# Where a transposed projection tile puts its 512-column and its 256-column products, and how the mixer's column tiles are summed

## The chip, the core and the metric

The kernel runs on one core of one Trainium2 chip. The metric is device time in microseconds (us) of one execution. The median of three runs of the kernel before is 892.92 us (892.76 to 893.49).

## What is computed

Two layers of a decoder trunk over 256 tokens (S) of 1024 channels (D). Each layer is a SwiGLU feed-forward block (FFN), a token mixer, and a second FFN, each followed by a layer norm:

```python
for l in range(DEPTH):                                   # DEPTH = 2, D_FF = 2816
    f = swiglu(x, ffn_w_gate[l, 0], ffn_w_up[l, 0], ffn_w_down[l, 0])
    x = layer_norm(ALPHA * x + 0.5 * f, ln_g[l, 0], ln_b[l, 0])
    z = x @ w_in[l]
    y_a = mixer_spatial_gating(z[..., :512], ...)        # heads A
    y_b = mixer_short_conv(z[..., 512:1280], ...)        # B: gate, gate, input
    y_c = mixer_rglru(z[..., 1280:], ...)                # C: gate, recurrent input
    y = jnp.concatenate([y_a, y_b, y_c], axis=-1) @ w_out[l]
    x = layer_norm(ALPHA * x + y, ln_g[l, 1], ln_b[l, 1])
    f = swiglu(x, ffn_w_gate[l, 1], ffn_w_up[l, 1], ffn_w_down[l, 1])
    x = layer_norm(ALPHA * x + 0.5 * f, ln_g[l, 2], ln_b[l, 2])
```

## The kernel before

**Arithmetic.** Every float32 operand is kept as two parts, a rounded high part and the rest as a low part, and a product is the sum of three: high by high, high by low and low by high. For weights the parts are the buffers `wh` and `wl`; for the activations, transposed so that channels lie on partitions, they are `xT[k, 0]` and `xT[k, 1]`, 256 columns each, side by side, for each of the KD = 8 blocks of 128 channels. `xTb` is the same tensor with both parts taken as one row of 512 columns.

**Weights.** They come from memory as blocks of 128 x 1024. For each block `stream` (L408) issues a DMA into one of 6 `raw` buffers, ScalarE rounds it into one of 12 `wh` buffers, and VectorE subtracts to fill the `wl` of the same number. So the two engines can be up to 12 blocks ahead of TensorE.

**Products with columns of weights (T tiles).** A block of 128 output channels is one tile: `sub_T` (L466) walks over the 8 values of k and calls a step that takes the weights as the stationary operand and `xT` as the moving one. There are two steps:

- `mm_TT` (L440), in the FFNs. A *joined* product of 512 columns (`wh` by both parts of `xT[k]`) fills a whole PSUM bank of 512 columns, and a *single* product of 256 columns (`wl` by the high part) adds to its first half. For k = 0 to 6 the joined one comes first; for k = 7 the two are swapped, so that the joined one closes the bank. Here J is a joined product and s a single one: a tile runs J s J s ... J s, then s J.
- `mm_T` (L434), in the mixers' column tiles: three products of 256 columns for each k, all into the first half of a bank.

In an FFN `total` (L452) then copies the second half of the bank out with ScalarE and adds the first half with VectorE. The 154 T tiles of the four FFNs are 40 in the first FFN and 38 in each of the others; the first FFN begins with `first_unit` (L625), which runs four tiles at once, one pair for each of four banks in turn, and the others begin with *nat* tiles (moving weights, activations stationary) and have two groups of three transposes among their first T tiles. After the T tiles comes `down` (L518): products of 512 columns into four banks, three for each block and half.

**Mixers.** Each of the two has 12 column tiles, made by `col` (L723) and used by `xr_sub`, `g_sub`, `c_sub`, `x_sub` and `b_sub`, which read the finished first half of the bank straight from PSUM. Among the column tiles stand `ri_sub` (L740), products of the convolved `xr`, `sgu` (L783), and transposes. The results go to `yTh` and `yTl`, the operands of the mixer's own `down`; its last input, channel block 7, is the result of `b_sub(1)`.

**Order.** The kernel records its operations with estimated costs, dependences and due times, and `issue` (L212) writes out one fixed order for each engine from them: TensorE by program order where operands are ready, VectorE and ScalarE by the earliest due time. Each engine then runs its list strictly in order. A product counts as columns plus 16, at 2.4 columns a nanosecond, whatever stands beside it.

Of the kernel before, what the change touches and what calls it, by code (L numbers as in the profile page):

```python
# [13 lines left out]
ALU = mybir.AluOpType  # L14
# [4 lines left out]
S = 256  # L19
L = 2  # L20
DFF = 2816
KD = D // P
# [256 lines left out]
def build(tc, a):  # L279
# [7 lines left out]
    def ap(v, dtype=None):  # L287
        return v.ap(dtype) if isinstance(v, View) else v
# [4 lines left out]
    def act(out, in_, func, scale=1.0, bias=0.0):  # L293
        ptrs = len(views(scale, bias))
        cost = in_.n / 1.2 + (50 if in_.psum else 92) + 93 * ptrs
        pr.add("A", cost, views(in_, scale, bias), [out], lambda: A.activation(  # L296
            out=ap(out), in_=ap(in_), func=func, scale=ap(scale), bias=ap(bias)))

    def tt(out, in0, in1, op, eng="V", as32=False, cost=None):
        cost = cost or out.n / 0.96 + 69  # L300
        e = V if eng == "V" else G
        pr.add(eng, cost, [in0, in1], [out], lambda: e.tensor_tensor(  # L302
            out=ap(out), in0=ap(in0), in1=ap(in1, F32 if as32 else None), op=op))
# [13 lines left out]
    def copy(out, in_):  # L317
        act(out, in_, AF.Copy)
# [5 lines left out]
    def walk(x):  # L324
        return x.rearrange("p (a b c) -> p b a c", b=RUNS, c=RUN)

    def mm(out, lhsT, rhs, start, stop, cost=None, runs=None, both=False):

        cost = cost or (out.n + 16) / 2.4

        def go():
            o, x = ap(out), ap(rhs)
            if runs is not None:
                x = walk(x)[:, runs]
                o = walk(o) if both else o
            T.matmul(out=o, lhsT=ap(lhsT), rhs=x, start=start, stop=stop)  # L336
        pr.add("T", cost, [lhsT, rhs], [out], go)
# [13 lines left out]
    def buf(name, shape, dtype=F32, pool=None, **kw):  # L351
        b = Buf(name, shape, dtype, phase=opened.get(pool), **kw)
        (cbufs if pool is None else phases[pool]).append(b)
        return b
# [21 lines left out]
    xT = buf("xT", (KD, 2, S), F32R, off=OFF_X)  # L376
    xTb = xT.alias((KD, 2 * S))
# [19 lines left out]
    def bank(*shape):  # L397
        b = bank_fifo.pop(0)
        return b.alias(shape) if shape else b
# [8 lines left out]
    def stream(upto, part=None):  # L408
        assert upto <= pos["blk"] + RING
        while loaded["n"] < min(upto, nblk):  # L410
            i = loaded["n"]
            r, h, l = raw[i % RAW], wh[i % RING], wl[i % RING]
            sl = slice(0, D) if part is None else slice(part * 512, part * 512 + 512)
            dma(r[sl], a["w"][i][:, sl])
            split(h[sl], l[sl], r[sl])
            if part == 0:
                return
            loaded["n"] += 1

    def take(n):  # L420
        b = pos["blk"]
        pos["blk"] += n
        stream(pos["blk"])
        return list(range(b, b + n))


    ALL = slice(0, RUNS)
# [12 lines left out]
    def mm_TT(b, h, l, k):  # L440


        def joined(stop):
            mm(b.all, h, xTb[k, :], k == 0, stop, runs=ALL, both=True)

        if k < KD - 1:
            joined(False)
        mm(b[:S], l, xT[k, 0, :], False, False, runs=ALL, both=True)
        if k == KD - 1:
            joined(True)  # L450

    def total(out, b):  # L452

# [12 lines left out]
    def sub_T(out, blk, step=mm_T):  # L466
        i = blk % RING
        for k in range(KD):
            ks = slice(k * P, (k + 1) * P)
            step(out, wh[i][ks], wl[i][ks], k)  # L470
# [91 lines left out]
    def ffn(layer, i, ln_prev, nxt, mid=None):  # L562
# [35 lines left out]
        for j, (kind, c0, n) in enumerate(units):  # L598
            if kind == "nat":
                continue  # L600
            f, m = c0 // P, n // P
            if kind == "first":
                first_unit(take(4), th, hh, hTh, hTl)
                continue
            b = take(2 * m)
            for q in range(m):
                pg = bank()
                sub_T(pg, b[q], mm_TT)
                total(hh[q, :], pg)
            act(th[:m, :], hh[:m, :], AF.Tanh, scale=0.5)  # L610
            stt(th[:m, :], th[:m, :], 1.0, hh[:m, :], ALU.add, ALU.mult)
            for _ in range(2):
                if todo:
                    hT(*todo.pop(0))
            for q in range(m):
                pu = bank()
                sub_T(pu, b[m + q], mm_TT)
                total(hh[q, :], pu)
            tt(hh[:m, :], th[:m, :], hh[:m, :], ALU.mult)
            split(hTh[f:f + m, :], hTl[f:f + m, :], hh[:m, :])  # L620
            if mid and j == 3:
                mid()
        return down(hTh, hTl, NF, TAIL, 4.0 * ALPHA, 16.0 * EPS, last, nxt)

    def first_unit(b, th, hh, hTh, hTl):  # L625

        accs = [bank() for _ in range(4)]
        for k in range(KD):
            i = b[k // 2] % RING
            for j in range(4):  # L630
                cs = slice((k % 2) * 512 + j * P, (k % 2) * 512 + (j + 1) * P)
                mm_TT(accs[j], wh[i][cs], wl[i][cs], k)
        for j in range(2):
            total(hh[j, :], accs[j])
            act(th[j, :], hh[j, :], AF.Tanh, scale=0.5)
            stt(th[j, :], th[j, :], 1.0, hh[j, :], ALU.add, ALU.mult)
            total(hh[j, :], accs[2 + j])
            tt(hh[j, :], th[j, :], hh[j, :], ALU.mult)
            split(hTh[j, :], hTl[j, :], hh[j, :])


    def mixer(layer, ln_prev, nxt):
# [3 lines left out]
        def mbuf(n, *shape, dtype=F32, **kw):  # L646
            return buf(n, shape, dtype, name, **kw)
# [15 lines left out]
        e2 = mbuf("e2", 4, S)  # L663
        cc = mbuf("cc", 2, S)
        cy = mbuf("cy", 2, S)
        gn = e2.alias((4, 256))
        vst = [mbuf(f"vst{h}", 6) for h in range(2)]
        vmv = [mbuf(f"vmv{h}", 2) for h in range(2)]
# [53 lines left out]

        def col():  # L723
            b = bank()
            sub_T(b[:S], take(1)[0])
            return b

        def g_sub(k):
            b = col()
            act(gT[k, :], b[:S], AF.Gelu_apprx_tanh)  # L730
            unbank(b)

        def xr_sub(k):
            b = col()
            act(xr[k, :], b[:S], AF.Identity, scale=pc(PW + k * 4 + 3), bias=pc(PB + k))
            for j in range(1, 4):
                stt(xr[k, j:], b[:S - j], pc(PW + k * 4 + 3 - j), xr[k, j:], ALU.mult, ALU.add)
            unbank(b)
# [25 lines left out]
        def c_sub(k):  # L764
            b = col()
            copy(cc[k, :], b[:S])
            unbank(b)
# [96 lines left out]
    b = bank()  # L864
# [15 lines left out]
    for layer in range(L):  # L880
        ln = ffn(layer, 0, ln, (layer, 1), derive if layer == 0 else None)
        ln = mixer(layer, ln, (layer, 2))
        ln = ffn(layer, 1, ln, (layer + 1, 0) if layer + 1 < L else None)
# [108 lines left out]
```

## Time and profile before

| | us |
|---|---|
| median of three runs | 892.92 |
| the profiled execution | 893.46 |
| its span, first to last instruction | 891.4 |
| TensorE (PE) busy | 882.3 |
| its weight loads (PEld) busy | 781.0 |
| VectorE (DVE) busy | 654.7 |
| ScalarE (ACT) busy | 483.9 |

The profiled execution lies 0.54 us above the median, and 2.06 us of it are outside the span. A product's "us" in the profile is from its start to its modelled end, which overlaps the next one's start; what a product costs the engine is the distance from its start to the start of the next. The timeline merges neighbours of one kind into one row (x2), so that the swap at the end of a tile shows as a row of two singles and a row of two joined ones.

### The profile page before, as it was taken

To read this page: it belongs to the slowest core of one execution; us is meant where nothing else is said; L and a number is where in the kernel's file an instruction comes from. 1 tells how busy PE (TensorE), PEld (TensorE's weight loads), DVE (VectorE), ACT (ScalarE), POOL (GpSimd) and SP (SyncE) were. 2 spreads that over 40 slices of the span, in tenths; PEclk is the share of its full clock that TensorE was granted. 3 is DMA by queue.
4 is the path that set the end of the run, shared out by engine and by line. 5 is a ranking of instruction groups with operands and counts; after the bars stand their busy time and mean duration, and the time that the engine had idled before them with its cause. 6 is when DMAs were issued, how large, how long until landed. Compare 5 with 4: busy or idle time off the path is not lost.

```text
span 891.4 us, 13272 instructions
## 1 busy us (share of the span) xinstructions
PE 882.3 (99%) x5068; PEld 781.0 (88%) x5068; DVE 654.7 (73%) x971; ACT 483.9 (54%) x707; POOL 22.3 (3%) x33
## 2 busy tenths in 40 slices
PE   9999999999999999999999999999999999999996
PEld 7888888889988888888888888888999888888885
DVE  6999775497898777764697777646979887777515
ACT  6785564267745656644455665543676466555410
POOL 0000000011000000000000000000200000000000
PEclk9999999999999999999999999999999999999999
DMA  8996555467358555555385555553853575555401
GB/s 311 375 314 228 190 192 205 171 221 252 118 187 277 198 189 189 191 206 194 131 281 202 190 195 193 201 190 125 320 208 112 195 271 190 194 201 195 142 1 47
DMA packets 51903, 178.11 MB, mean 200 GB/s; under 512 B 6144, under 2 KB 7936, under 8 KB 51840
## 3 DMA queue, kind: packets, MB, share of 16 engines
q1 hardware_dynamic: 51840, 177.28, 57.3%
q8 instruction: 39, 0.64, 0.3%
q14 instruction: 24, 0.20, 0.1%
HBM read 176.20 MB, written 1.05 MB: 199 GB/s over the span
## 4 chain that ended last, share of the span: by engine, by line
PE 97%; DMA 1%; DVE 1%; SPq 0%; ACT 0%; issue 0%; DVEq 0%
PE bank L336 96%; PE bank L340 1%; DMA raw<-w 1%; DMA x0t<-xT 1%; SPq L346 0%; DVE xn L314 0%; DVE wl L302 0%; ACT wh L296 0%; DVE st L488 0%; DVEq L988 0%; DVE mv L493 0%; DVE ve L309 0%
## 5 line engine op out<-in xcount | busy, mean ns | idle before, releaser
L302 DVE TENSOR_TENSOR wl<-raw,wh 128x1024 fp32r<-128x1024 f32 (+1 forms) x320 | 385.5, 1209 | 155.2 <-ACT wh L296 154.0
L336 PE MATMUL bank<-xT,wh 128*128 128x512 f32 (+1 forms) x1648 | 492.8, 363 | 0.2 <-DVE xT L302 0.2
L296 ACT ACTIVATE wh<-raw 128x1024 fp32r<-128x1024 f32 (+1 forms) x320 | 333.8, 1048 | 235.2 <-PE bank L336 218.4
L336 PE MATMUL bank<-xT,wl 128*128 128x256 f32 x1456 | 377.8, 277 | 0.4 <-DVE wl L302 0.4
L336 PEld LDWEIGHTS bank<-xT,wh 128*128 128x128 f32 x1648 | 285.4, 188 | 38.8 <-DVE xT L302 0.9
L336 PEld LDWEIGHTS bank<-xT,wl 128*128 128x128 f32 x1456 | 273.7, 188 | 12.5 <-DVE wl L302 1.3
L336 PE MATMUL bank<-wl,hTh 128*128 128x512 f32 (+1 forms) x374 | 138.2, 369 | 0.0
L336 PE MATMUL bank<-wh,hTh 128*128 128x512 f32 (+1 forms) x374 | 137.9, 369 | 0.0
L336 PE MATMUL bank<-wh,hTl 128*128 128x512 f32 (+1 forms) x374 | 137.9, 369 | 0.0
L296 ACT ACTIVATE hh<-bank 128x256 f32<-128x256 f32 x158 | 56.5, 374 | 78.2 <-PE bank L336 73.5
L302 DVE TENSOR_TENSOR hh<-bank,hh 128x256 f32<-128x256 f32 x158 | 64.2, 419 | 26.7 <-ACT hh L296 26.6
L336 PEld LDWEIGHTS bank<-wl,hTh 128*128 128x128 f32 x374 | 70.2, 188 | 10.8
L336 PEld LDWEIGHTS bank<-wh,hTh 128*128 128x128 f32 x374 | 70.3, 188 | 10.7
L336 PEld LDWEIGHTS bank<-wh,hTl 128*128 128x128 f32 x374 | 70.2, 188 | 10.6
L336 PE MATMUL bank<-wh,xT 128*128 128x512 f32 (+1 forms) x320 | 79.3, 334 | 0.0
L336 PEld LDWEIGHTS bank<-wh,xT 128*128 128x128 f32 x320 | 54.9, 188 | 6.5 <-DVE xT L302 0.6
L336 PE MATMUL bank<-wl,xT 128*128 128x512 f32 (+1 forms) x160 | 53.0, 331 | 0.0
L314 DVE SCALAR_TENSOR_TENSOR xn<-xn,bank 128x512 f32<-128x512 f32 (+1 forms) x25 | 16.2, 663 | 38.2 <-PE bank L336 38.2
L302 POOL TENSOR_TENSOR rs<-ve,mhalf 128x1 f32<-128x1 f32 x16 | 13.8, 863 | 863.5 <-DVE ve L309 863.5
L336 PEld LDWEIGHTS bank<-wl,xT 128*128 128x128 f32 x160 | 30.1, 188 | 3.1
L296 ACT ACTIVATE hTh<-hh 128x512 fp32r<-128x512 f32 (+1 forms) x42 | 25.4, 605 | 8.4 <-DVE hh L302 8.2
L302 DVE TENSOR_TENSOR hh<-th,hh 128x512 f32<-128x512 f32 (+1 forms) x42 | 27.7, 660 | 1.2
(93 smaller groups left out, 470.3 us busy)
## 6 DMA issues: line engine op xcount, KB each, us to landing
raw<-w SPq DMA_DIRECT2D x312, 512.0 KB, 4.1
gB<-ln_g SPq DMA_DIRECT2D x6, 512.0 KB, 6.5
bB<-ln_b SPq DMA_DIRECT2D x6, 512.0 KB, 6.4
raw<-w SPq DMA_DIRECT2D x8, 256.0 KB, 5.1
x0t<-xT SPq DMA_DIRECT2D x8, 128.0 KB, 4.6
xn<-x SPq DMA_DIRECT2D x2, 512.0 KB, 6.1
out<-xn SPq DMA_DIRECT2D x3, 256.0 KB, 2.0
wT<-sgu_wT SPq DMA_DIRECT2D x2, 256.0 KB, 6.8
```

What stands on the lines that cost most here:

```text
L296: pr.add("A", cost, views(in_, scale, bias), [out], lambda: A.activation(out=ap(out), in_=ap(in_), func=func, scale=ap(scale), bias=ap(bias)))
L302: pr.add(eng, cost, [in0, in1], [out], lambda: e.tensor_tensor(out=ap(out), in0=ap(in0), in1=ap(in1, F32 if as32 else None), op=op))
L314: pr.add("V", cost, views(in0, s, in1), [out], lambda: V.scalar_tensor_tensor(out=ap(out), in0=ap(in0), scalar=ap(s), in1=ap(in1), op0=op0 ...
L336: T.matmul(out=o, lhsT=ap(lhsT), rhs=x, start=start, stop=stop)
L340: pr.add("T", 109.0, [in_, ident.all], [out], lambda: T.transpose(out=ap(out), in_=ap(in_), identity=ap(ident.all)))
```

## The change

`mm_TT` loses its swap: every k issues the joined product, then the single one, and the closing mark moves to the single one of k = 7. The mixers' `col` uses `mm_TT` instead of `mm_T`. Since its result then lies in both halves of the bank and its users read the first half alone, ScalarE copies the second half into a new buffer `low` of 256 columns (one for all twelve tiles), and VectorE adds it onto the first half, in PSUM.

```diff
     def mm_TT(b, h, l, k):
-        def joined(stop):
-            mm(b.all, h, xTb[k, :], k == 0, stop, runs=ALL, both=True)
-
-        if k < KD - 1:
-            joined(False)
-        mm(b[:S], l, xT[k, 0, :], False, False, runs=ALL, both=True)
-        if k == KD - 1:
-            joined(True)
+        mm(b.all, h, xTb[k, :], k == 0, False, runs=ALL, both=True)
+        mm(b[:S], l, xT[k, 0, :], False, k == KD - 1, runs=ALL, both=True)
...
+        low = mbuf("low", S)
...
         def col():
             b = bank()
-            sub_T(b[:S], take(1)[0])
+            sub_T(b, take(1)[0], mm_TT)
+            copy(low.all, b[S:])
+            tt(b[:S], b[:S], low.all, ALU.add)
             return b
```

In the built program, TensorE around the end of a T tile of the first FFN (the bank's name changes where the next tile begins; 32x4 is the joined product, 16x4 the single one), before:

```order
L336 MATMUL bank_103<-xT,wh_86 128x4x32x4
L336 MATMUL bank_103<-xT,wl_98 128x4x16x4 x2
L336 MATMUL bank_103<-xT,wh_86 128x4x32x4
L336 MATMUL bank_104<-xT,wh_75 128x4x32x4
L336 MATMUL bank_104<-xT,wl_87 128x4x16x4
```

and, as a piece of the difference at the end of the four interleaved tiles of `first_unit`:

```order
+L336 MATMUL bank_100<-xT,wh_78 128x4x32x4
 L336 MATMUL bank_100<-xT,wl_90 128x4x16x4
-L336 MATMUL bank_100<-xT,wh_78 128x4x32x4
+L336 MATMUL bank_101<-xT,wh_78 128x4x32x4
 L336 MATMUL bank_101<-xT,wl_90 128x4x16x4
```

The neighbouring two singles and the two joined products are gone everywhere; TensorE's products alternate without a break.

VectorE in the first mixer, around the convolution of the second `xr` tile (bank_103; bank_105 is the column tile g3, `wl` are weight splits), before:

```order
L302 TENSOR_TENSOR wl_89<-raw_70,wh_77 128x1024
L314 SCALAR_TENSOR_TENSOR xr<-bank_103,prm,xr 128x255
L314 SCALAR_TENSOR_TENSOR xr<-bank_103,prm,xr 128x254
L314 SCALAR_TENSOR_TENSOR xr<-bank_103,prm,xr 128x253
L302 TENSOR_TENSOR wl_90<-raw_71,wh_78 128x1024
```

and after:

```order
L302 TENSOR_TENSOR bank_103<-bank_103,low 128x256
L314 SCALAR_TENSOR_TENSOR xr<-bank_103,prm,xr 128x255
L302 TENSOR_TENSOR bank_105<-bank_105,low 128x256
L314 SCALAR_TENSOR_TENSOR xr<-bank_103,prm,xr 128x254
L302 TENSOR_TENSOR wl_90<-raw_71,wh_78 128x1024
L314 SCALAR_TENSOR_TENSOR xr<-bank_103,prm,xr 128x253
```

The three multiply-adds on `xr` stood together, ahead of the split; now an addition for a later tile and the split stand between them.

VectorE at the end of the first mixer (cc and cy belong to the B heads, bank_104 and bank_101 are the two `b_sub` tiles), before:

```order
L314 SCALAR_TENSOR_TENSOR cy<-cc,prm,cy 128x255
L302 TENSOR_TENSOR yTl<-cc,yTh 128x256
L314 SCALAR_TENSOR_TENSOR cy<-cc,prm,cy 128x254
L302 TENSOR_TENSOR wl_97<-raw_72,wh_85 128x1024
L302 TENSOR_TENSOR cc<-cy,bank_101 128x256
L302 TENSOR_TENSOR wl_98<-raw_73,wh_86 128x1024
L302 TENSOR_TENSOR yTl<-cc,yTh 128x256
```

and after:

```order
L314 SCALAR_TENSOR_TENSOR cy<-cc,prm,cy 128x255
L302 TENSOR_TENSOR cc<-cy,bank_104 128x256
L314 SCALAR_TENSOR_TENSOR cy<-cc,prm,cy 128x254
L302 TENSOR_TENSOR bank_101<-bank_101,low 128x256
L302 TENSOR_TENSOR yTl<-cc,yTh 128x256
L302 TENSOR_TENSOR cc<-cy,bank_101 128x256
L302 TENSOR_TENSOR wl_97<-raw_72,wh_85 128x1024
L302 TENSOR_TENSOR yTl<-cc,yTh 128x256
```

The added addition stands ahead of the last `yTl`, and one weight split has moved behind it.

## Rows read from the trace of the kernel before

**Rows 1.** The page: span, and busy time of each engine.

```profile
span 891.4 us, 13272 instructions
PE 882.3 (99%) x5068; PEld 781.0 (88%) x5068; DVE 654.7 (73%) x971; ACT 483.9 (54%) x707; POOL 22.3 (3%) x33
...
PE 97%; DMA 1%; DVE 1%; SPq 0%; ACT 0%; issue 0%; DVEq 0%
```

**Rows 2.** Waits of PE: for whom, total us, times, longest.

```profile
PE bank L336 <- DVE zero L863: 1.3, 1, 1.3
PE bank L336 <- DVE wl L302: 0.4, 2, 0.2
```

**Rows 3.** Groups by line and shape: xcount | busy us, mean ns | idle.

```profile
L336 PE MATMUL bank<-xT,wh 128*128 128x512 f32 x1264 | 424.3, 388 | 0.2 <-DVE xT L302 0.2
L336 PE MATMUL bank<-xT,wh 128*128 128x256 f32 x384 | 68.6, 280 | 0.0
```

**Rows 4.** Timeline of PE, first FFN (start, us, engine, line, operation).

```profile
100.27 0.28 PE L336 MATMUL bank<-xT,wl 128*128 128x256 f32 x1
100.38 0.38 PE L336 MATMUL bank<-xT,wh 128*128 128x512 f32 x1
100.60 0.28 PE L336 MATMUL bank<-xT,wl 128*128 128x256 f32 x1
...
102.27 0.39 PE L336 MATMUL bank<-xT,wl 128*128 128x256 f32 x2
102.50 0.64 PE L336 MATMUL bank<-xT,wh 128*128 128x512 f32 x2
102.97 0.28 PE L336 MATMUL bank<-xT,wl 128*128 128x256 f32 x1
...
103.44 0.40 PE L336 MATMUL bank<-xT,wh 128*128 128x512 f32 x1
103.67 0.28 PE L336 MATMUL bank<-xT,wl 128*128 128x256 f32 x1
...
105.29 0.60 PE L336 MATMUL bank<-xT,wh 128*128 128x512 f32 x2
...
107.96 0.64 PE L336 MATMUL bank<-xT,wh 128*128 128x512 f32 x2
```

**Rows 5.** Timeline of PE in first_unit, and the first wait behind it.

```profile
13.05 0.28 PE L336 MATMUL bank<-xT,wl 128*128 128x256 f32 x1
...
15.13 0.28 PE L336 MATMUL bank<-xT,wl 128*128 128x256 f32 x1
...
18.20 0.38 PE L336 MATMUL bank<-xT,wl 128*128 128x256 f32 x1 [0.16 <-DVE wl L302]
```

**Rows 6.** Timeline of PE, second FFN: after three transposes.

```profile
284.62 0.28 PE L336 MATMUL bank<-xT,wl 128*128 128x256 f32 x1
...
285.98 0.28 PE L336 MATMUL bank<-xT,wl 128*128 128x256 f32 x1
...
286.65 0.39 PE L336 MATMUL bank<-xT,wl 128*128 128x256 f32 x2
...
287.35 0.28 PE L336 MATMUL bank<-xT,wl 128*128 128x256 f32 x1
...
289.10 0.28 PE L336 MATMUL bank<-xT,wl 128*128 128x256 f32 x1
```

**Rows 7.** Timeline of PE: the first mixer's last two column tiles, and down.

```profile
236.39 0.39 PE L336 MATMUL bank<-xT,wh 128*128 128x256 f32 x2
...
239.14 0.39 PE L336 MATMUL bank<-xT,wh 128*128 128x256 f32 x2
...
241.89 0.38 PE L336 MATMUL bank<-wh,yTh 128*128 128x512 f32 x1
```

**Rows 8.** Groups by shape: a copy and an addition as the change adds them.

```profile
L296 ACT ACTIVATE hh<-bank 128x256 f32<-128x256 f32 x158 | 56.5, 374 | 78.2 <-PE bank L336 73.5 <-DVE hTl L302 2.1 <-DVE sp L309 1.2
L302 DVE TENSOR_TENSOR hh<-bank,hh 128x256 f32<-128x256 f32 x158 | 64.2, 419 | 26.7 <-ACT hh L296 26.6
```

**Rows 9.** The first mixer's column tiles: us, busy of PE, PEld, DVE, ACT.

```profile
203.51:241.89 38.38, 38.38 (x322) 37.95 (x321) 29.70 (x56) 27.82 (x46) 3.75 (x4) 1.00 0.53 185
```

**Rows 10.** Timeline of DVE, then of PE: two results and their users.

```profile
214.19 1.51 DVE L314 SCALAR_TENSOR_TENSOR xr<-bank,prm,xr 128x255 f32<-128x255 f32 x3
...
249.37 0.42 DVE L302 TENSOR_TENSOR yTl<-cc,yTh 128x256 fp32r<-128x256 f32 x1
...
218.64 0.59 PE L336 MATMUL bank<-xr,wa 128*128 128x256 f32 x2
...
250.91 0.38 PE L336 MATMUL bank<-wh,yTl 128*128 128x512 f32 x1
```

## The prediction, made before the changed kernel ran

> **What bounds the kernel now.** I read the busy shares first, then PE's waits, then the starts of single products. PE is busy for 882.3 of 891.4 us, and the chain that ended last is PE for 97% [rows 1]. It waits for next to nothing: 1.3 us for the first zeros and 0.4 us for weights at the start [rows 2]. So a product's column count, and what two neighbouring products do to each other, set the time; the other engines matter only where they come late. What the reader must see is the distance between starts. In one T tile joined products start 0.22 us and singles 0.11 us before their successors (100.27, 100.38, 100.60), and the six pairs from 100.27 to 102.27 take 2.00 us, 0.3333 us each [rows 4]. In the next tile a joined product takes 0.23 to 0.24 us (103.44 to 103.67) without any wait. The rows of two joined products stand 2.79 us apart across the slow tile (102.50 to 105.29) and 2.67 us across the fast one (105.29 to 107.96), 5.46 us for two tiles, and this alternation runs on to the end of each FFN: of the 154 T tiles 74 are slow, 69 fast and 11 irregular (beside transposes, or the first ones of an FFN).
>
> **When a tile turns slow.** It turns at the swap. Two singles in a row pass at once, and the two joined products behind them (102.50 to 102.97) take 0.47 us where twice 0.22 would be 0.44 [rows 4]; from there the pairs stay slow until the next swap throws them back. In the fast tile all pairs between the swaps keep 0.3333 us exactly. So there are at least two steady ways to run the same pair; a swap kicks PE out of the good one, and the next one happens to kick it back. After any other disturbance the good one is found within a few pairs: behind three transposes the four pairs from 284.62 to 285.98 take 1.36 us, 0.03 over, and from there PE keeps the good pace up to the swap at 286.65 [rows 6]. Ten such entries stand in the trace (one in the first FFN, three in each of the others); all reach the good pace within 8 pairs.
>
> **Term 1, the FFNs.** The change removes the swaps and adds no instruction. If the good pace, once found, lasts across tiles, a tile costs 8 x 0.3333 = 2.667 us. Two tiles then take 5.333 us instead of 5.46: 69 slow-fast couples give 69 x 0.127 = 8.8 us. The five slow tiles beyond these give about 0.11 each, 0.6 us, and the irregular ones lose a swap or one late entry, 0.2 us (an estimate from the 0.03 us of the joined pair at the swap). That is 9.5 us. Nothing behind it becomes late: VectorE and ScalarE wait for PE to free weight buffers, not the other way [rows 2], and 1% more pace is far from their busy shares [rows 1]. What could break the pace at a tile's border is the new bank and the jump back from k = 7 to 0; the swapped border has both as well, and behind a slow tile it begins the good pace (105.29), so I price them at nothing.
>
> A rule speaks against this whole term. The Trainium skill, "TensorE: Matmul & The Clock Gate", in "Part 2: What happens when you issue a matmul", says that the next weights are loaded through a read port of their own and take no bandwidth from the running product. By that rule 512 and 256 columns would cost the same in any order and term 1 would be zero. The trace disagrees as far as two tiles of equal columns and no wait differ by 0.12 us [rows 4], though it does not show why.
>
> **Term 2, PE in the mixers' column tiles.** 384 products of 256 columns, two for each of 24 x 8 pairs [rows 3], become 192 of 512, and singles stay. An undisturbed column tile takes 2.75 us now (236.39 to 239.14 to 241.89) [rows 7] against 2.667: 24 x 0.083 = 2.0 us. Seven of twelve tiles begin behind something else (transposes, `ri_sub`, `sgu`, the nat tiles) and pay the entry of 0.03 to 0.04 us: 14 x 0.035 = 0.5 us. Net gain 1.5 us; bounds 0 (if none finds the pace) and 2.0.
>
> **Term 3, the sum put back.** Each column tile adds a copy on ACT, 374 ns, and an addition on DVE, 419 ns by the same shape from PSUM to SBUF [rows 8]; none here writes PSUM, so I take 0.42 with 0.35 and 0.6 as ends. Over 38.38 us of column tiles ACT goes from 27.8 to 32.3 us and DVE from 29.7 to 34.7 [rows 9], 84% and 90%: it fits in total. It lengthens each chain from a column tile by 0.8 to 0.9 us, and the queues are strict. Two places are tight. The second `xr` was ready at 214.19 + 1.51 = 215.70 and used at 218.64 [rows 10], 2.9 us of slack. Now its last multiply-add stands behind the addition for g3 and a weight split: from g3's end about 0.45 (copy) + 0.42 + 0.48 + 1.22 + 0.48 = 3.1 us, and PE comes to it after one `ri_sub` and one tile, 0.67 + 2.86 = 3.5 us. Just covered. The last `yTl` was ready at 249.79 and used at 250.91, 1.1 us of slack [rows 10]. Its list on DVE has an addition and a multiply-add more ahead of it and one split less, and starts some 0.4 us later behind ScalarE's three added copies, while PE arrives 0.2 us earlier. I work this out to a stall of 0.2 to 0.4 us; with the other tight joints I take 0.4 us in each mixer, 0.8 in all, bounds 0 and 3. The three splits pushed behind are needed tens of us later. A bank is held 0.8 us longer, of eight, with a tile each 2.7 us: nothing.
>
> **The sum.** 9.5 + 1.5 - 0.8 = 10.2 us off the profiled execution's 893.46 gives 883.3; off the median, 0.54 lower, 882.7 us. With the bounds of terms 2 and 3 on the good side, and 0.3 us more for term 1 (its rows are rounded to 0.01 us), 881.1; with terms 2 and 3 on the bad side 886.4.
>
> **Rivals.**
>
> *The slow steady pace everywhere.* The only place of before where J and s alternate for longer than a tile is `first_unit`, and there six pairs from 13.05 to 15.13 take 2.08 us, 0.3467 each, steadily, until the swaps end it [rows 5]. If the changed stream ran so, 154 tiles would take 154 x 2.773 = 427.1 us against 421.6 now (74 x 2.78 + 69 x 2.68 + 11 irregular ones of 2.8 on average), 5.5 us more; mixers gain nothing and stall 0.8: 899.2 us, slower. It decides if an FFN's last entry lands there; then no swap frees it. Against it: ten of the eleven entries reached the good pace. For it: the pattern is the very one.
>
> *The slow pace in one or two of the four FFNs.* Each costs 34 tiles x 8 x 0.0133 = 3.6 us: 886.3 or 889.9 us.
>
> *The pace is lost at every border and found again.* Then each tile pays something between 0.03 us [rows 6] and the slow tile's 0.11, much what the mean tile pays today (5.46 / 2 - 2.667 = 0.063): 892 us, from 887 to 900.
>
> *Order is not the cause.* Slow tiles could follow the odd-numbered weight buffers, which they mostly do. Then terms 2 and 3 alone remain, 892.2 us. This is also where the skill's rule above leads. Against it, in the second FFN the tile that by the built order uses weight buffer 4 is a slow one, five pairs from 287.35 to 289.10 in 1.75 us [rows 6], where in the first FFN even buffers are fast; the step sits at the swap, not with the buffer.
>
> **How the numbers follow.** The forecast 62%, 881.1 to 886.4. The slow pace in one or two FFNs 14%. Lost at the borders 12%, split over faster, same and slower as 5, 3 and 4. The slow pace everywhere 8%, order not the cause 4%. A measurement of this kernel tells about 0.2%, 1.8 us, from no change: faster 62 + 14 + 5 = 81%, same 3 + 4 = 7%, slower 4 + 8 = 12%. The range that holds 8 in 10 runs from 881.1 to 891.0, the forecast, the partly slow case and the better half of the border case.
>
> **What the profile of after would show.** Right: the starts of the first singles of consecutive T tiles 2.67 us apart all along, no row x2 of joined products in a T tile, 107 us for the first FFN's T tiles, column tiles of 2.67 us, PE waiting below 1 us in a mixer. Wrong: pairs of 0.347 us in long runs (the slow pace), or 0.3333 broken at each change of bank. Waits of PE for `xr` or `yTl` over 0.5 us would break term 3. The clock was granted in full in that stretch, 1.00 [rows 9]; a lower one would void all of it.

## The result: 882.28 us, a ratio of 0.9884

| | before | after |
|---|---|---|
| median of three runs, us | 892.92 (892.76 to 893.49) | 882.28 (882.01 to 883.76) |
| the profiled execution, us | 893.46 | 883.76 |
| its span, us | 891.4 | 881.7 |

The ratio is 0.9884, with a 95% interval of 0.9861 to 0.9906. The forecast was 882.7 us. The profiled execution of the changed kernel is the slowest of its three; for it the sum gave 883.3 us.

The page of the changed kernel, span and busy times, beside [rows 1]:

```profile
span 881.7 us, 12928 instructions
PE 872.1 (99%) x4876; PEld 770.9 (87%) x4876; DVE 658.5 (75%) x995; ACT 491.4 (56%) x731; POOL 22.3 (3%) x33
```

TensorE still bounds the kernel. It has 192 instructions fewer (384 products of 256 columns became 192 of 512) and 10.2 us less busy time. Its waits (for whom, total us, times, longest), beside [rows 2]:

```profile
PE bank L336 <- DVE zero L860: 1.2, 1, 1.2
PE bank L336 <- DVE wl L302: 0.7, 2, 0.5
PE bank L336 <- DVE xT L302: 0.4, 1, 0.4
```

Next the timeline of TensorE in the first FFN (start, us, engine, line, operation), beside [rows 4]. Three tiles begin at 99.75, 102.42 and 105.08; the second pair of the first begins at 100.08. No row of that stretch shows x2 any more:

```profile
99.75 0.38 PE L336 MATMUL bank<-xT,wh 128*128 128x512 f32 x1
...
100.08 0.38 PE L336 MATMUL bank<-xT,wh 128*128 128x512 f32 x1
...
102.42 0.38 PE L336 MATMUL bank<-xT,wh 128*128 128x512 f32 x1
...
105.08 0.38 PE L336 MATMUL bank<-xT,wh 128*128 128x512 f32 x1
...
107.75 0.38 PE L336 MATMUL bank<-xT,wh 128*128 128x512 f32 x1
```

A pair takes 0.33 us and eight of them 2.667 (99.75 to 107.75 is 24 pairs in 8.00 us), where the swaps at the ends of a slow and a fast tile stood 2.79 and 2.67 apart [rows 4]. Where the time went is shown by the stretches of T tiles in the four FFNs, from the first tile behind `first_unit` or the first T tile to the first product of `down` (us, then busy us and count of PE, PEld, DVE, ACT and POOL, granted clock, DMA share, GB/s), before:

```profile
17.66:127.36 109.70, 109.54 (x641) 96.73 (x640) 98.43 (x176) 73.91 (x116) 0.00 (x0) 1.00 0.77 270
281.32:385.75 104.43, 104.43 (x616) 92.58 (x615) 78.90 (x110) 61.47 (x98) 0.00 (x0) 1.00 0.59 204
461.89:566.39 104.50, 104.50 (x616) 92.65 (x615) 78.91 (x110) 61.48 (x98) 0.00 (x0) 1.00 0.60 204
720.32:824.75 104.43, 104.43 (x616) 92.61 (x615) 78.90 (x110) 61.47 (x98) 0.00 (x0) 1.00 0.59 205
```

and after, with the column tiles of the first mixer as a last line:

```profile
17.58:125.08 107.50, 107.00 (x642) 96.34 (x641) 98.19 (x176) 74.81 (x116) 0.00 (x0) 1.00 0.79 278
278.64:380.85 102.21, 102.21 (x617) 92.26 (x616) 78.08 (x111) 61.60 (x98) 0.00 (x0) 1.00 0.59 209
457.01:559.17 102.16, 102.16 (x617) 92.24 (x616) 78.08 (x110) 61.53 (x98) 0.00 (x0) 1.00 0.60 209
712.87:815.04 102.17, 102.17 (x617) 92.22 (x615) 78.06 (x111) 61.56 (x98) 0.00 (x0) 1.00 0.59 208
...
201.23:238.91 37.68, 37.68 (x227) 33.88 (x226) 30.97 (x63) 30.70 (x57) 3.80 (x5) 1.00 0.55 188
```

The four FFNs lose 2.20, 2.22, 2.34 and 2.26 us, 9.0 together, with the same products and the same clock. The mixer's tiles lose 38.38 - 37.68 = 0.70 us [rows 9]. The added operations, by shape (count, busy us, mean ns, idle before them), beside [rows 8]:

```profile
L302 DVE TENSOR_TENSOR bank<-bank,low 128x256 f32<-128x256 f32 x24 | 10.2, 424 | 0.8 <-ACT low L296 0.8
...
L296 ACT ACTIVATE low<-bank 128x256 f32<-128x256 f32 x24 | 9.0, 375 | 3.5 <-DVE ra L302 1.9 <-DVE bank L302 1.6
```

### The profile page after: what moved, and what is told of

It reads as the page before. It is cut to its first block, busy times and chain, and to the rows that moved or that the text cites. A ratio compares the mean times of both kernels' runs of the same rounds, so it can differ in the third digit from the quotient of the medians.

```text
span 881.7 us, 12928 instructions
## 1 busy us (share of the span) xinstructions
PE 872.1 (99%) x4876; PEld 770.9 (87%) x4876; DVE 658.5 (75%) x995; ACT 491.4 (56%) x731; POOL 22.3 (3%) x33
## 4 chain that ended last, share of the span: by engine, by line
PE 97%; DMA 1%; DVE 1%; SPq 0%; ACT 0%; issue 0%; DVEq 0%
PE bank L336 96%; PE bank L340 1%; DMA raw<-w 1%; DMA x0t<-xT 1%; SPq L346 0%; DVE xn L314 0%; DVE wl L302 0%; ACT wh L296 0%; DVE st L482 0%; DVEq L985 0%; DVE mv L487 0%; DVE ve L309 0%
## 5 line engine op out<-in xcount | busy, mean ns | idle before, releaser
L336 PE MATMUL bank<-xT,wh 128*128 128x512 f32 x1456 | 491.0, 383 | 0.4 <-DVE xT L302 0.4
L336 PE MATMUL bank<-xT,wl 128*128 128x256 f32 x1456 | 401.1, 276 | 0.7 <-DVE wl L302 0.7
L336 PEld LDWEIGHTS bank<-xT,wh 128*128 128x128 f32 x1456 | 273.6, 188 | 48.8 <-DVE xT L302 1.1
L336 PEld LDWEIGHTS bank<-wh,hTl 128*128 128x128 f32 x374 | 70.2, 188 | 10.6
L336 PEld LDWEIGHTS bank<-wl,hTh 128*128 128x128 f32 x374 | 70.2, 188 | 10.6
L302 DVE TENSOR_TENSOR hh<-bank,hh 128x256 f32<-128x256 f32 x158 | 59.7, 417 | 0.0
L296 ACT ACTIVATE hh<-bank 128x256 f32<-128x256 f32 x158 | 51.4, 373 | 5.2 <-DVE hTl L302 2.6
```

## The experiments

All FFN edits below are in `mm_TT`; J is the joined product, s the single one.

### The two halves of the change apart

`e1_ffn_only`: no swap in the FFNs, the mixers as before.

```diff
         def col():
             b = bank()
-            sub_T(b, take(1)[0], mm_TT)
-            copy(low.all, b[S:])
-            tt(b[:S], b[:S], low.all, ALU.add)
+            sub_T(b[:S], take(1)[0])
             return b
```

> The FFNs lose the swap, the mixers keep three products of 256 columns and no added sum. My theory (nearly all of the gain is the FFN tiles, which keep the good pace of 0.3333 us a pair once they have it; the mixers give some 0.5 us each after their stall): 883.2 us, within 882.8 to 883.7, and all late T tiles of an FFN at 2.667 us. Rival (the mixers' part carries a good share of the 10.6 us): over 885 us.

Measured: 884.1 us against 893.4, ratio 0.9899 (0.9883 to 0.9914). Nearly the whole gain is the FFNs'. In its trace the first mixer's column tiles take 38.34 us, 0.66 more than in the changed kernel; in medians the mixers' part (884.1 to 882.28, not measured side by side) is too small for the intervals to tell.

`e2_mixer_only`: the mixers as changed, the swap kept in every T tile.

```diff
+        def joined(stop):
+            mm(b.all, h, xTb[k, :], k == 0, stop, runs=ALL, both=True)
+        if k < KD - 1:
+            joined(False)
+        mm(b[:S], l, xT[k, 0, :], False, False, runs=ALL, both=True)
+        if k == KD - 1:
+            joined(True)
```

> The mixers get the joined products and the added sum, but every tile keeps the swap of its last pair, the FFNs too. My theory (the swap is what makes tiles slow): the undisturbed column tiles come out at 2.67 to 2.78 us instead of 2.75, the stall at the last input of the mixer's down stays, so 892.4 to 893.2 us, no gain. Rival (joining products gives the mixers' gain by itself): 891.9 us or less.

Measured: 894.5 us, ratio 1.0012 (1.0002 to 1.0021), above the range expected. The stretch of the same 12 tiles takes 38.65 us here, 0.27 more than before, but the tiles' own products aren't the reason: by the distances between starts they take 33.70 us, where they took 33.99 before and take 33.23 in the changed kernel. Instead TensorE stalls for 0.54 us at the four transposes of `un`, which VectorE finishes late in this version. These transposes, before and here:

```profile
233.16 0.60 PE L340 MATMUL bank<-ident,un 128*128 128x128 f32 x4
...
233.70 1.14 PE L340 MATMUL bank<-ident,un 128*128 128x128 f32 x4
```

So the joined products alone shorten a mixer's tiles by 0.3 us, and the stall takes more than that back; without the swap they are 0.65 to 0.76 shorter. One tile keeps a slow pace from its second pair up to its swap:

```profile
213.34 0.39 PE L336 MATMUL bank<-xT,wh 128*128 128x512 f32 x1
...
215.07 0.39 PE L336 MATMUL bank<-xT,wh 128*128 128x512 f32 x1
```

From 213.34 to 215.07 five pairs take 1.73 us, 0.346 each: the slow pace of `first_unit` [rows 5].

### Which part of the swap breaks the pace

`e3_extra_single`: a tile ends J s s, so two singles follow each other, two joined ones never.

```diff
+        if k == KD - 1:
+            mm(b[:S], l, xT[k, 0, :], False, True, runs=ALL, both=True)
```

> As the changed kernel, with the last single product of every tile issued twice (the low part of k = 7 counts double in the output), so two products of 256 columns stand in a row at each tile's end, and never two of 512. 182 tiles x 0.1133 = 20.6 us are the plain cost: 902.9 us and 2.78 us a T tile if only two joined products in a row break the pace (theory J). If two singles in a row break it (theory S), each T tile pays 0.05 to 0.11 us more: 2.83 to 2.89 us, 912 to 923 us.

Measured: 917.61 us, of which 5.2 are waits for `xr` in the mixers. TensorE at the ends of three tiles:

```profile
100.04 0.39 PE L336 MATMUL bank<-xT,wl 128*128 128x256 f32 x2
100.27 0.40 PE L336 MATMUL bank<-xT,wh 128*128 128x512 f32 x1
100.50 0.28 PE L336 MATMUL bank<-xT,wl 128*128 128x256 f32 x1
...
102.89 0.39 PE L336 MATMUL bank<-xT,wl 128*128 128x256 f32 x2
...
105.71 0.39 PE L336 MATMUL bank<-xT,wl 128*128 128x256 f32 x2
```

The tiles take 2.85 and 2.82 us in turn, where 2.667 and a single of 0.113 make 2.78. So two singles in a row are enough to disturb it: the J behind them takes 0.23 us (100.27 to 100.50). The good pace returns within the tile.

`e4_extra_joined`: the last J is doubled, which adds its product twice to the output.

```diff
+        if k == KD - 1:
+            mm(b.all, h, xTb[k, :], False, False, runs=ALL, both=True)
```

> As the changed kernel, with the joined product of k = 7 of every tile issued twice (it counts double in the output), so two products of 512 columns stand in a row at each tile's end, and never two of 256. 182 x 0.220 = 40.0 us are the plain cost: 922 to 923 us and 2.887 us a T tile if only two singles in a row break the pace (theory S, as the run with an extra single showed that they do break it). If two joined ones in a row break it as well (theory J), T tiles come out at 2.93 us or more, 930 us or more.

Measured: 932.19 us, 9 above what harmless pairs of J would give. The doubled J of one tile of the first FFN, then of two tiles of the second:

```profile
101.45 0.60 PE L336 MATMUL bank<-xT,wh 128*128 128x512 f32 x2
...
102.00 0.38 PE L336 MATMUL bank<-xT,wh 128*128 128x512 f32 x1
102.22 0.28 PE L336 MATMUL bank<-xT,wl 128*128 128x256 f32 x1
...
320.23 0.60 PE L336 MATMUL bank<-xT,wh 128*128 128x512 f32 x2
...
320.79 0.40 PE L336 MATMUL bank<-xT,wh 128*128 128x512 f32 x1
321.02 0.28 PE L336 MATMUL bank<-xT,wl 128*128 128x256 f32 x1
...
323.20 0.60 PE L336 MATMUL bank<-xT,wh 128*128 128x512 f32 x2
```

In the first FFN every J behind the pair takes 0.22 us, and a tile is 2.887, which is 2.667 and one J. In the other three the next J takes 0.23 and a tile 2.967. So whether two joined products in a row disturb the pace isn't settled by their order alone; why the FFNs differ stays open.

### Is the slow tile a lasting pace or a passing one?

`e5_rare_swap`: the swap in every fourth T tile only.

```diff
+        swap = k == KD - 1 and count["n"] % 4 == 3
+        if not swap:
+            mm(b.all, h, xTb[k, :], k == 0, False, runs=ALL, both=True)
+        mm(b[:S], l, xT[k, 0, :], False, k == KD - 1 and not swap, runs=ALL, both=True)
+        if swap:
+            mm(b.all, h, xTb[k, :], k == 0, True, runs=ALL, both=True)
```

> As the changed kernel, but every fourth T tile has the swap of its last pair back (45 of 182 tiles). Theory that the slow pace is a steady state, as I wrote it in the prediction (a swap throws PE out, only the next one throws it back): four slow tiles follow four fast ones, about 91 slow tiles x 0.11 = 10 us, 892 us. Theory that it is a transient (PE finds the good pace by itself within 8 to 10 pairs, as behind transposes): one slow tile behind each swap, then three at 2.667 us: 45 x 0.12 = 5 us at most, 885 to 888 us.

Measured: 889.79 us. Four tiles in a row, the first one with the swap (columns: us, busy of PE, clock, DMA share, GB/s):

```profile
102.29:104.97 2.68, 2.68 (x18) 1.00 0.59 199
104.97:107.77 2.80, 2.80 (x18) 1.00 0.56 187
107.77:110.45 2.68, 2.68 (x18) 1.00 0.63 193
110.45:113.12 2.67, 2.67 (x18) 1.00 0.62 196
```

Behind a swap one tile is slow, the next gets back to 2.667 without another swap, and then it stays. So the slow tile of before was a passing disturbance about nine pairs long. A swap costs 0.16 us in every place of this run beyond the entries, not the 0.06 by which a mean tile of before exceeded 2.667: there every second swap came when the pace was still lost.

### Do addresses matter, or only the order?

`e6_shift_x` and `e8_before_x0` move only `xT`, the moving operand, 16 bytes lower (four float32), the first in the changed kernel and the second in the kernel before. `e9_shift_x8` sets the offset to 8 and was meant to move it 16 bytes higher, but `allocate` takes the offset modulo 8, so that 8 lays `xT` where 0 does: e9 is the program of e6 once more, and a shift upward wasn't tested.

```diff
-OFF_X = 4
+OFF_X = 0
```

> As the changed kernel, with the activations xT 16 bytes lower in every partition, weights and all else where they were. Theory that the pace is set by reads that meet (the moving columns of one product and the weight load of the next, in the same part of the memory at the same time): the pairs of the T tiles leave 0.3333 us, by an amount that I can't work out, 0.335 to 0.36 us, so 885 to 915 us. Theory that the pace is a matter of the queue and the load's length alone (addresses play no part): every late T tile stays at 2.667 us, 882 to 883 us.

> The changed kernel with xT laid 16 bytes higher (e6 laid it 16 bytes lower). Theory (places of reads decide): the tiles of the FFNs take some steady length other than 2.667 us; nothing in the rows says whether below it, where columns alone would be 2.56, or above it, like the 2.693 of e6, and I expect above, 2.69, 886.5 us. Rival (e6's loss came from something else that its layout moved): 2.667 and 882.3 us.

> The kernel before, with xT laid 16 bytes lower as in e6. Theory (the length of a product depends on where its columns' reads meet those of the next weights): the good pace there is 0.3367 us a pair instead of 0.3333, so fast tiles take about 2.70 instead of 2.68, and the slow ones change by another amount; in all 0 to 4 us above the kernel before, not the same as it. Rival (the shift only matters to the alternation without swaps): slow and fast tiles stay at 2.78 and 2.68 and the time stays within 0.5 us.

Measured, one execution each: 886.63 (e6) and 887.72 us (e9) for the changed kernel with `xT` shifted, 891.12 for the one before (893.57 unshifted, measured beside it). In both executions of the shifted changed kernel every T tile beyond the entries takes 2.693 us, 0.027 more than unshifted. The shifted kernel before:

```profile
102.46 0.39 PE L336 MATMUL bank<-xT,wl 128*128 128x256 f32 x2
...
105.17 0.39 PE L336 MATMUL bank<-xT,wl 128*128 128x256 f32 x2
...
107.88 0.39 PE L336 MATMUL bank<-xT,wl 128*128 128x256 f32 x2
```

Its tiles take 2.71 us each by these rows, so that it is faster than the kernel before and slower than the changed one. My expectation of 0 to 4 us above was wrong in sign: the steady pace is worse there, but the swap hardly disturbs it. The whole change is worth 10.6 us at the address as it is and 3.4 to 4.5 us 16 bytes lower (891.12 to 887.72 and 886.63); in the T stretches of the four FFNs alone it is worth 9.0 and 2.3 us. So the cost of an order depends on where the moving operand lies. This would fit reads that meet, of the moving columns and the next weights, but no run here shows what meets, so the cause stays open.

The Trainium skill, "TensorE: Matmul & The Clock Gate", "Part 2: What happens when you issue a matmul", says that loading the next weights takes no read bandwidth from the running product. No run here tests that sentence by itself; a tile of the same products that goes from 2.667 to 2.693 us with a shift of 16 bytes speaks against using it as a rule for time.

### What the sum put back costs

`e7_no_sum`: the changed kernel without the copy and the addition.

```diff
-            copy(low.all, b[S:])
-            tt(b[:S], b[:S], low.all, ALU.add)
```

> The changed kernel without the copy and the addition in the mixers' column tiles: the low part times the high weights, in the second half of the bank, is left out of the mixers' output. TensorE's products are the same. Theory: the sum put back costs TensorE only the stall of about 0.25 us at the last yTl of each mixer, so 0.5 us less than the changed kernel, 881.8 us, and the mixers' column tiles keep the lengths they have there (2.67 undisturbed, 2.73 to 2.93 behind other work). Rival: the additions, which write PSUM while TensorE writes other banks, also slow the products: then the tiles behind other work shrink to 2.67 and it is 881 or less.

Measured: 882.48 us, ratio 0.9875 (0.986 to 0.9889), which isn't to be told from the changed kernel's 0.9884. The trace does tell: the last `yTl` of the first mixer and its user. First the changed kernel, DVE and then PE, then DVE without the sum:

```profile
247.59 0.42 DVE L302 TENSOR_TENSOR yTl<-cc,yTh 128x256 fp32r<-128x256 f32 x1
...
247.71 0.39 PE L336 MATMUL bank<-wl,yTh 128*128 128x512 f32 x1
248.06 0.49 PE L336 MATMUL bank<-wh,yTl 128*128 128x512 f32 x1
248.39 0.38 PE L336 MATMUL bank<-wh,yTh 128*128 128x512 f32 x1
```

```profile
246.30 0.42 DVE L302 TENSOR_TENSOR yTl<-cc,yTh 128x256 fp32r<-128x256 f32 x1
```

With the sum `yTl` is ready at 248.01, and the two products from 247.71 take 0.68 us where twice 0.22 would be 0.44: a stall of about 0.25 us, which isn't listed as a wait. Without the sum it is ready at 246.72 and the stall is gone. The column tiles keep their lengths, so additions that write PSUM beside the products cost TensorE nothing that can be seen.

`e10_last_plain`: two edits meant to take the stall away. `b_sub(1)` uses `mm_T` and no sum (`col(True)` is the old `col`); the c tiles sum straight into `cc`.

```diff
         def c_sub(k):
-            b = col()
-            copy(cc[k, :], b[:S])
-            unbank(b)
+            b = bank()
+            sub_T(b, take(1)[0], mm_TT)
+            total(cc[k, :], b)
         def b_sub(k):
-            b = col()
+            b = col(k == 1)
```

> The changed kernel with two edits that keep the sum off the path: the last column tile of each mixer, b_sub(1), goes back to three products of 256 columns and needs no sum, and the c tiles write their sum straight into cc, which saves a copy. Theory: in each mixer the stall of 0.25 us at the last yTl goes, and the plain tile gives 0.08 to 0.12 us back: 0.3 us less in all, 882.0 us, which three rounds hardly tell from the changed kernel. Rival: the plain tile loses the pace for what follows, and the time is the changed kernel's or up to 0.5 us above it.

Measured: 884.98 us (884.17 to 887.85), ratio 0.9901 (0.9884 to 0.9917). The edits fail, by one line of its waits:

```profile
PE bank L336 <- DVE yTl L302: 1.0, 2, 0.5
```

The written order counted on an earlier result: on VectorE two weight splits of 1.22 us, where the changed kernel has one, now stand among the last steps to that `yTl` (at 245.36 and 247.16 in e12, the same program). The two products around it take 1.23 us there, where they took 0.68 in the changed kernel. The spans of e12 and the changed kernel differ by 1.2 us (882.9 and 881.7), 1.0 of it in the two stretches from a mixer's column tiles to the next FFN; the rest of the 2.7 us between the medians isn't explained. The profiled execution, 887.85 us, shows something else as well, told next.

### Several steady paces

In that execution every T tile of the first FFN took 2.773 us, the rival price of the prediction to the nanosecond, and the other FFNs 2.667. TensorE's products up to there are the same list as in the changed kernel. So `e12_last_plain_again` runs the kernel of e10 once more, and `e11_one_swap` puts one swap into its fourteenth joined tile, the tenth behind `first_unit`:

```diff
+        swap = k == KD - 1 and count["n"] == 13
```

> The kernel of e10 once more, nothing changed. Theory (the pace of the first FFN is chosen in each execution by when the first weights come): it may begin with tiles of 2.667 or of 2.773 us; where TensorE waits 0.5 us or more for wl behind first_unit, as in the changed kernel, it is 2.667 and the time about 884; where it comes just in time, 2.773 and 887 to 888. Rival (these edits themselves make the first FFN slow, whose instructions they leave as they were): 2.773 again, whatever TensorE waits for.

> The kernel of e10 with one swap alone: in the first FFN, at the end of the tenth tile behind first_unit. In e10 that whole FFN ran pairs of 0.3467 us. Theory (two steady paces, and which one holds is set by how the first product behind first_unit meets its weights; a swap throws PE out of either, and the good one follows): if the FFN again begins with tiles of 2.773 us, they end at this swap, and the tiles from the twelfth on take 2.667; about 29 x 0.106 = 3.1 us less than e10, 884.8 us. If it begins with 2.667, one tile behind the swap takes about 2.79 and nothing else changes, 883 to 884 us. Rival (the slow pace comes from something lasting in that execution, memory traffic or the chip): tiles of 2.773 go on behind the swap, 887 us or more.

Measured: 884.92 us for e12, 885.1 for e11. The T tiles of the first FFN from the second one behind `first_unit` on, in e10:

```profile
19.59:127.74 108.15, 108.15 (x626) 95.60 (x625) 96.09 (x172) 71.75 (x112) 0.00 (x0) 1.00 0.74 265
```

and in e12, the same program:

```profile
20.99:124.99 104.00, 104.00 (x627) 93.92 (x625) 94.71 (x172) 71.42 (x111) 0.00 (x0) 1.00 0.78 272
```

39 tiles differ by 4.15 us at the same clock; the whole times differ by less (887.85 and 884.92), because e10 saves the wait shown below. The first product behind `first_unit` and its neighbours, in e10:

```profile
16.80 0.40 PE L336 MATMUL bank<-xT,wh 128*128 128x512 f32 x1
17.04 0.29 PE L336 MATMUL bank<-xT,wl 128*128 128x256 f32 x1
```

and in e12:

```profile
17.36 0.40 PE L336 MATMUL bank<-xT,wh 128*128 128x512 f32 x1
18.39 0.38 PE L336 MATMUL bank<-xT,wl 128*128 128x256 f32 x1 [0.62 <-DVE wl L302]
```

In e12, as in the profiles of e1, e7, e11 and the changed kernel, TensorE waits 0.5 to 0.7 us there for the first split of a full block, and the good pace follows. In e10 the weights came earlier and the products met them without a listed wait; the first J took 0.24 us and the slow pace followed to the end of the FFN. So both paces belong to one program, and each lasted from the entry on. What picks one stays open. A missing wait alone doesn't: in e4, behind its doubled J's, TensorE met the weights of this place without a wait too, and from there on every J took 0.22 us. There the split had ended 0.81 us before its first single product (17.70 and 18.51); in e10 it ended 0.16 us before (16.88 and 17.04):

```profile
15.65 1.23 DVE L302 TENSOR_TENSOR wl<-raw,wh 128x1024 fp32r<-128x1024 f32 x1 [1.18 <-ACT wh L296]
```

That weights coming just in time start the slow pace is a guess from this one slow entry against five good ones. In e11 the FFN's tiles began in the good pace, so whether a swap ends the slow one wasn't tested; its swap cost 0.06 us (2.671 and 2.721 for two tiles), where the same swap cost 0.16 in e5, and no run shows why.

There is a third steady pace. In `first_unit` of e11, whose products are the same list as in the changed kernel, 18 pairs take 6.12 us, 0.340 each, until the wait behind them:

```profile
11.21 0.39 PE L336 MATMUL bank<-xT,wh 128*128 128x512 f32 x1
...
17.33 0.39 PE L336 MATMUL bank<-xT,wh 128*128 128x512 f32 x1
```

The changed kernel held 0.3333 there, and the kernel before, with the same list up to its swaps, 0.3467 [rows 5].

No version here beats the changed kernel.

## Why the prediction was right, step by step

**What bounds the kernel.** Right: the saving came from the distances between starts alone, with waits of 1.2, 0.7 and 0.4 us.

**Term 1, 9.5 us.** Right in mechanism and size: 9.0 us measured in the four stretches. Of the 0.5 us too many 0.33 are the first tile behind `first_unit`, which took 3.507 us where it had taken 3.174. TensorE came to it only 0.08 us earlier (17.58 against 17.66), but the weight split that it waits for there ended 0.28 us later (18.42 against 18.14), behind a block that landed later. I had not asked who feeds this tile. Most of the rest is the count of tiles: by the distances between first products 73 were slow, 67 fast and 14 irregular, not 74, 69 and 11. The tile's border cost nothing, as priced.

**When a tile turns slow.** The observation was right, the explanation partly wrong. I wrote that pairs stay slow until the next swap throws them back. Experiment e5 shows that the pace returns without it after about nine pairs; the next swap only came before that. A lasting slow pace exists as well (`first_unit` of before, the first FFN of e10), which the rival had from [rows 5], but the slow tiles of before weren't it. The sum survived since both readings give 2.667 us without swaps. The ground for expecting all four FFNs in the good pace was ten of eleven entries of before; that the profiled execution got it in all four is in part luck.

**Term 2, 1.5 us.** 0.70 us in the first mixer; in the second 38.34 us (starts 642.58 to 680.92) became 37.74 (635.33 to 673.07), 0.60. That is 1.3 together. Undisturbed tiles take 2.667, as said; those behind other work 2.73 to 2.93 (before 2.75, and up to 2.95). What the disturbed ones take beyond the undisturbed grew by 0.24 and 0.35 us a mixer, about the 7 x 0.035 that was priced.

**Term 3, 0.8 us.** 0.7 us: the stretches from a mixer's last column tile to the next FFN's first T tile grew by 0.30 and 0.40 (39.43 to 39.73, 39.40 to 39.80). Of this 0.25 and 0.22 are the stall at the last `yTl`, inside the 0.2 to 0.4 that the text worked out; the rest is spread over small differences. No wait for the second `xr` is listed. The addition into PSUM took 424 ns for 0.42 assumed, the copy 375 for 374.

**The sum.** 9.0 + 1.3 - 0.7 = 9.6 us, with 0.1 more ahead of the first stretch; the spans differ by 9.7, and 10.2 was forecast. The medians differ by 10.6, so that the median came out 0.4 us below its forecast and the profiled execution 0.5 above: being this close is in part luck.

**The rivals.** "Order is not the cause" is refuted by e1 and e3: at fixed addresses the order alone moves every tile. "Lost at every border" by the rows of after. "The slow pace in one or two FFNs" is real: it happened in one FFN of one profiled execution of e10, at 39 x 0.106 = 4.15 us where I had priced 3.6 for 34 tiles; the wait that this entry saved brought the loss down to about 3 us. The changed kernel carries this risk too, since its list there is the same; its three times show none of that size.

## What to carry to other kernels

When an engine is 99% busy, read the distance between starts, not the busy time of an instruction: equal products here cost 0.220 to 0.239 us by the order around them, by an address and by the entry, and an alternation without the swap at each tile's end was worth 1.0% (e1). Price an order together with the addresses it was measured at, since a shift of 16 bytes changed the worth of the same edit from 10.6 us to between 3.4 and 4.5. Look at the built address, not at the constant that is meant to set it: an offset of 8 here was an offset of 0. And where the pace has more than one steady value, look at several executions and at the entry of each loop.

## What I had not expected of the hardware

- The same list of products on TensorE, in two executions of one program at a granted clock of 1.00, held pairs of 0.3333 us for a whole FFN in one and 0.3467 in the other (104.00 and 108.15 us for 39 tiles). A third program held 0.340 for 18 pairs of the list that the changed kernel ran at 0.3333.
- Laying the moving operand 16 bytes lower changed the steady pair from 0.3333 to 0.3367 us on average, and made the swap nearly harmless (with it tiles of 2.71 us against 2.73 unshifted, without it 2.693 against 2.667).
- Two short products in a row cost 0.04 to 0.07 us in the products behind them (e3); two long ones nothing in one FFN and 0.08 us a tile in three others (e4).
